# A streaming-encoder block on one core: when VectorE reads a shared PSUM bank, and how many filler products stand ahead of two places

## The chip, the cores and the metric

The kernel runs on 1 core of a Trainium2 chip. Its time is device microseconds of one execution; the time before is the median of 3 runs, 795.69 us (795.49 to 801.71). The profile is of one further execution, which took 797.75 us; its span, from the first to the last instruction in the trace, is 796.0 us.

## The reference, cut to what matters

One layer of a hybrid block: x is 512 rows of 1024. One projection gives queries, keys and values for two kinds of attention with eight heads each, an indexer and two gates.

```python
def block(args):                        # sparse heads ("a"), per 128 rows
    dots = einsum('thd,sd->ths', qib, k_idx) * IDX_DIM ** -0.5
    score = einsum('th,ths->ts', wib, relu(dots))       # indexer score
    _, sel = top_k(where(chunk ok, score, -inf), 128)   # keys each row may see
    logits = q . k[sel] * HEAD_DIM ** -0.5 + bias[bucket(sel - t)]
    return softmax(logits) @ v[sel]

a = exp(log_sigmoid(z) + later)         # stick-breaking heads ("s"): later is a
return a @ v                            # reverse running sum of log_sigmoid(-z)

x = layer_norm(ALPHA * x + merged @ w_out)              # then a gated conv MLP
```

## The kernel before, in words

All matrix work is done in pairs of high and low float parts: a weight tile of 128 x 1024 comes in by DMA from SP's queue (line 66), ScalarE makes its high part (line 93), VectorE, or GpSimd for some tiles, its low part (line 95), and TensorE then makes three products per tile of 128 (high by high, high by low, low by high; for projections lines 201 to 203, for values 224 to 226). Stream.get keeps three pieces ahead.

The phases are: a start in which the indexer's queries are projected as x arrives; the attention phase; the output projection and first norm; the MLP (lines 739 to 741 and 768 to 770); the last norm. The change touches the attention phase alone.

In that phase the order of TensorE's instructions is written by hand (manual_schedule); the order on the other engines is set by the scheduler when the program is built. The attention work of TensorE is small and waits on the other engines, so between its pieces the code puts **fillers**: products of projections, values and the branch output which are needed anyway, taken in one fixed sequence (FILL) from a generator. fill(n) issues fillers until n products are out; each step is three products, so n is rounded up to a multiple of three, and fill(16) issues 18. The total number of fillers is fixed: what is not issued at one place comes at a later one, and fill(9999) issues the rest.

The phase runs thus:

- idx_keys projects the indexer's key (ki) and splits it into kih (ScalarE, line 332) and kil (VectorE, line 333). idx_scores issues 24 pairs of products dot_ps (lines 352 and 353; the second reads kil), with fill(3) ahead of each; ScalarE takes the relu (355), VectorE adds it to score (358, 360).
- select(j) finds the 128 highest of a row of score in 16 rounds of two VectorE operations (369, 370). These rounds are spread over the fillers, and those left are issued ahead of the first sparse head.
- Sixteen heads follow, eight "s", then eight "a". For a head, start_head issues its score products (8 of them: z_ps, line 433, or l_ps, line 471), then come fill(gap), turn_weights for the head **before** (10 transposes tr_ps, line 391, then ScalarE pth 395 and VectorE ptl 396), fill(gap), weigh for that head (8 products av_ps, line 407, which read pth and ptl), and fill(gap). So a head's score products stand about 54 fillers ahead of its own transposes.
- For an s head ScalarE reads z_ps twice (keep 437, beta 438), VectorE runs the running product over keep (447) and GpSimd multiplies beta by it (449).
- For an a head VectorE adds the bias and the mask bm (made by GpSimd, line 460, from score) to l_ps and takes the row's minimum mn (475), ScalarE takes the exponential (477), VectorE scales by the reciprocal sum (480, 483).
- A pair of heads needs its queries qs and keys ks (or qa, ka): ScalarE and VectorE write their parts, and ScalarE's queue issues a DMA for the queries (306 to 308), which waits for VectorE's part.

Scores of a head lie in three PSUM banks: block 3 (512 columns) in one, **blocks 0 and 2 (128 and 384 columns) together in one**, block 1 (256) in one. These banks, those of tr_ps and that of av_ps come from one ring of four (psB); a ring place is used again only when its last reader is done.

Of the kernel before, what the change touches and what calls it, by code (L numbers as in the profile page):

```python
# [42 lines left out]
OFF = {0: 0, 2: 128, 3: 512, 1: 1024}  # L43
# [3 lines left out]
def r32(ap):  # L47
    return ap.bitcast(F32)
# [59 lines left out]
def tile_block(ctx: ExitStack, tc: tile.TileContext, xT, xN, w_qi, w_ki, w_t, w_v, w_br, w_o, w_fi, w_fo,  # L108
               bg, cw, rel, onehot, lnp, out):
    nc = tc.nc  # L110
# [8 lines left out]
    def padded(pool, shape, dt=F32, **kw):  # L119

        n = int(np.prod(shape[1:]))
        t = pool.tile([shape[0], -(-n // 32) * 32], dt, **kw)[:, :n]
        return t if len(shape) == 2 else t.rearrange("p (a b) -> p a b", a=shape[1])
# [11 lines left out]
    def pa(name):  # L135
        return psA.tile([128, 512], F32, tag="A", name=name)

    def pb(name):
        return psB.tile([128, 512], F32, tag="B", name=name)
# [36 lines left out]
    ps = pb("idle_ps")  # L176
# [80 lines left out]
    for k in range(KC):  # L257
# [9 lines left out]
        for n in range(4):  # L267
            c = slice(n * 128, n * 128 + 128)
# [56 lines left out]
    def idx_keys():  # L325
        ps = whole(proj_t("ki", M=72))
        kih = bp.tile([128, 512], F32R, tag="pt", bufs=8, name="kih")
        kil = bp.tile([128, 512], F32R, tag="pt", bufs=8, name="kil")
        wiT = bp.tile([8, 512], F32, tag="pt", bufs=8, name="wiT")
        nc.scalar.activation(wiT, ps[64:72], AF.Copy, scale=float(H) ** -0.5)  # L330
        for r in (slice(0, 64), slice(64, 128)):
            nc.scalar.activation(kih[r], ps[0:64], AF.Copy)
            nc.vector.tensor_sub(kil[r], ps[0:64], r32(kih[0:64]))
        wi = padded(cst, [128, 3, H], name="wi")
        fill(12)
        ps = pa("wi_ps")
        for j in (1, 2, 3):
            nc.tensor.transpose(ps[:, (j - 1) * H:j * H], wiT[:, j * 128:j * 128 + 128], ident[:H, :H])
        nc.vector.tensor_copy(wi.rearrange("p a b -> p (a b)"), ps[:, :3 * H])
        index["k"] = kih, kil, wi  # L340
# [3 lines left out]
    def idx_scores():  # L344
        kih, kil, wi = index["k"]
        for j in (1, 2, 3):
            N = 128 * (j + 1)
            for h in range(H):
                yield j
                ps = pa("dot_ps")  # L350
                r = slice(j * 128, j * 128 + 128)
                nc.tensor.matmul(ps[:, :N], qi[h][:, r], kih[:, :N], start=True, stop=False)
                nc.tensor.matmul(ps[:, :N], qi[h][:, r], kil[:, :N], start=False, stop=True)
                rl = bp.tile([128, 512], F32, tag="pt", bufs=8, name="relu")
                nc.scalar.activation(rl[:, :N], ps[:, :N], AF.Relu, scale=0.125)
                w = wi[:, j - 1, h:h + 1]
                if h == 0:
                    nc.vector.tensor_scalar(score[j], rl[:, :N], w, None, op0=ALU.mult)
                else:
                    nc.vector.scalar_tensor_tensor(score[j], rl[:, :N], w, score[j], op0=ALU.mult, op1=ALU.add)  # L360
# [15 lines left out]
    def select_some(n):  # L376
        for _ in zip(range(n), rounds):
            pass
# [74 lines left out]
    def dsa_head(q, k, h):  # L453
        win = bp.tile([128, 512], F32, tag="win", bufs=2, name="win")
        nc.sync.dma_start(win, s_win[h])
        nc.gpsimd.memset(win[0:64, 448:512], BIG)
        bm = padded(bp, [128, ATT + 1], tag="keep", bufs=2, name="bm")
        for j in (1, 2, 3):
            N = 128 * (j + 1)
            nc.gpsimd.tensor_add(bm[:, OFF[j]:OFF[j] + N], win[:, 512 - N:512], score[j])  # L460
        lg = bp.tile([128, ATT], F32, tag="beta", bufs=2, name="lg")
        mn = padded(bp, [128, NB], tag="mn", bufs=2, name="mn")
        sm = padded(bp, [128, NB], tag="sm", bufs=2, name="sm")
        rs = padded(bp, [128, NB], tag="rs", bufs=2, name="rs")
        for grp in ((3,), (0, 2), (1,)):
            ps = pb("l_ps")
            o = 0
            for j in grp:
                N = 128 * (j + 1)
                for hl in range(2):  # L470
                    nc.tensor.matmul(ps[:, o:o + N], q[:, hl, j * 128:j * 128 + 128], k[:, :N],
                                     start=(hl == 0), stop=(hl == 1))
                c = slice(OFF[j], OFF[j] + N)
                b = win[:, 384:512] if j == 0 else bm[:, c]
                nc.vector.tensor_tensor_reduce(out=lg[:, c], in0=ps[:, o:o + N], in1=b, scale=1.0, scalar=3.0e38,
                                               op0=ALU.add, op1=ALU.min, accum_out=mn[:, j:j + 1])
                nc.scalar.activation(lg[:, c], lg[:, c], AF.Exp, scale=-1.0, bias=mn[:, j:j + 1],
                                     accum_out=sm[:, j:j + 1])
                o += N
        nc.vector.reciprocal(rs, sm)  # L480
        for j in range(NB):
            c = slice(OFF[j], OFF[j] + 128 * (j + 1))
            nc.vector.tensor_scalar(lg[:, c], lg[:, c], rs[:, j:j + 1], None, op0=ALU.mult)
        return lg
# [45 lines left out]
    def fill(n, every=0):  # L530

        step = 0
        while n > 0:
            c = next(fillers, None)
            if c is None:
                return
            n -= c
            step += 1
            if every and step % every == 0:
                select_some(1)  # L540

    def fill_until(*keys):
        while not all(k in done for k in keys):
            fill(1)
# [5 lines left out]
    with tc.manual_schedule(engines={nc.tensor.engine}):  # L550
        fill(12)
        idx_keys()

        oh = bp.tile([64, NREL], F32R, tag="beta", bufs=2, name="oh")
        rb = edge.tile([64, H], F32R, name="rb")
        nc.gpsimd.tensor_copy(oh, ohf)
        nc.vector.tensor_copy(rb[0:32], rbf)
        nc.vector.tensor_sub(rb[32:64], rbf, r32(rb[0:32]))
        line = bp.tile([H, NREL], F32, tag="beta", bufs=2, name="line")
        for a, b in ((0, 512), (512, NREL)):  # L560
            ps = pa("line_ps")
            nc.tensor.matmul(ps[:H, :b - a], rb, oh[:, a:b], start=True, stop=True)
            nc.scalar.activation(line[:, a:b], ps[:H, :b - a], AF.Copy, scale=-1.0)
        s_line = nc.dram_tensor("s_line", (H, NREL), F32, kind="Internal").ap()
        s_win = nc.dram_tensor("s_win", (H, 128, 512), F32, kind="Internal").ap()
        nc.gpsimd.dma_start(s_line, line)
        nc.gpsimd.dma_start(s_win, bass.AP(tensor=s_line.tensor, offset=s_line.offset + 127,
                                           ap=[[NREL, H], [-1, 128], [1, 512]]))

        for j in idx_scores():  # L570
            if j > 1:
                select_some(1)
            fill(3)
# [10 lines left out]
    with tc.manual_schedule(engines={nc.tensor.engine}):  # L584
        fill_until("qs0", "ks0")
        fill(15)
        weights = start_head(0)
        sb_sticks(*weights)
        fill_until("qs1", "ks1")
        for i, (w, h) in enumerate(heads):  # L590
            gap = GAP[w]
            following = start_head(i + 1) if i + 1 < len(heads) else (None,)
            fill(gap)
            pth, ptl, lows = turn_weights(weights[0])
            if len(following) == 2:
                with tc.issue_after(lows):
                    scan = sb_sticks(*following)
                with tc.issue_after(scan):
                    select_some(1)
                fill(gap, 3)  # L600
            else:
                fill(gap)
            if h % 2 == 0:
                ytmp = bp.tile([128, 512], F32, tag="yt", bufs=2, name=f"y{w}t{h//2}")
            weigh(pth, ptl, vals[w], h, ytmp)
            if h % 2 == 1:
                (ys if w == "s" else ya).append(finish_pair(ytmp, f"y{w}{h//2}"))
            fill(gap, 3 if i < H - 1 else 0)
            weights = following
# [30 lines left out]
    for p in range(4):  # L640
        wh_wl = st.get(f"ba{p}")
        for n in (2 * p, 2 * p + 1):
            if n not in early and n not in gps:
                gps[n] = whole(proj_t(f"ga{n}"))
            ps = pb("ba_ps")
            wh, wl = wh_wl
            for k in range(4):
                c = slice((n % 2) * 512 + k * 128, (n % 2) * 512 + k * 128 + 128)
# [290 lines left out]
```

## Time and profile before

| what | value |
|---|---|
| median of 3 runs | 795.69 us |
| profiled execution | 797.75 us, span 796.0 us |
| TensorE (PE) busy | 772.2 us, 97% |
| VectorE (DVE) busy | 485.3 us, 61% |
| ScalarE (ACT) busy | 326.6 us, 41% |
| GpSimd (POOL) busy | 118.0 us, 15% |
| mean granted TensorE clock | 0.994 |
| longest wait of TensorE, by group | l_ps L471 on DVE mn L475, 10.6 us in 8 times |

In the views a line such as "PE L471 MATMUL l_ps<-ka0a,qa0a" names the engine, the line of the kernel, the operation and the tiles written and read. "[2.08 <-DVE mn L475]" behind it is the idle time of the engine just before it and the instruction that ended this idle time. The view of stretches gives, for each window of time, the busy time of PE, PE's weight loads, DVE, ACT and POOL with the number of instructions, then the granted TensorE clock (1.00 is full speed), the DMA share and the rate. In the timeline neighbouring equal instructions stand in one row with their number (x4), at the start of the first.

### The profile page before, as it was taken

The numbers are of one execution on the slowest core, as the hardware profiler recorded it, in microseconds if no ns is written. First come the engines' busy times: TensorE is split into PE (matmuls) and PEld (weight loads), VectorE is DVE, ScalarE is ACT, GpSimd is POOL, SyncE is SP. The second block draws the span as 40 slices with busy tenths as digits, with TensorE's granted clock in tenths as the row PEclk, the third lists the DMA queues.
The fourth block names the chain that finished last, engine by engine and source line by source line (L and its number), as shares of the span: only waits on it lengthen the run. The fifth ranks groups of instructions, "written<-read, shape, count | busy, mean of one in ns | idle before, by whom it ended". The sixth has DMA issues, their size and how long they took to land.

```text
span 796.0 us, 9705 instructions
## 1 busy us (share of the span) xinstructions
PE 772.2 (97%) x3696; PEld 647.0 (81%) x3696; DVE 485.3 (61%) x782; ACT 326.6 (41%) x514; POOL 118.0 (15%) x123
## 2 busy tenths in 40 slices
PE   8999999999889999999999999999999999999996
PEld 6878788888777778878889888888888888888885
DVE  5679797899657775538864554354435344545345
ACT  5565556545445547625411433333323322423300
POOL 0012464537611211000101000000000000000002
PEclk9999999999999999999999999999999999999999
DMA  7354323232212331115801332232223232231402
GB/s 253 142 182 138 96 90 107 75 113 87 85 67 93 106 119 64 69 54 174 344 11 54 107 106 86 88 119 85 100 80 112 100 106 80 105 106 57 156 26 80
DMA packets 26591, 84.01 MB, mean 106 GB/s; under 512 B 3816, under 2 KB 4200, under 8 KB 26544
## 3 DMA queue, kind: packets, MB, share of 16 engines
q1 hardware_dynamic: 22320, 72.87, 26.6%
q10 hardware_dynamic: 2576, 6.29, 2.9%
q0 software_dynamic: 1648, 4.22, 1.5%
q8 instruction: 29, 0.48, 0.2%
q14 instruction: 18, 0.15, 0.1%
HBM read 77.06 MB, written 4.21 MB: 102 GB/s over the span
## 4 chain that ended last, share of the span: by engine, by line
PE 87%; DVE 9%; ACT 1%; issue 1%; DMA 1%; POOL 0%; POOLq 0%; ACTq 0%; SPq 0%; DVEq 0%
PE d_ps L769 5%; PE d_ps L770 5%; PE d_ps L768 5%; PE u_ps L741 5%; PE u_ps L739 5%; PE g_ps L741 5%; PE u_ps L740 5%; PE g_ps L739 5%; PE g_ps L740 5%; DVE keep L447 2%; PE av_ps L407 2%; PE ga_ps L201 2%; PE ga_ps L203 2%; PE ga_ps L202 2%; PE o_ps L700 2%; PE o_ps L699 2%
## 5 line engine op out<-in xcount | busy, mean ns | idle before, releaser
L95 DVE TENSOR_TENSOR wlo<-raw,whi 128x1024 fp32r<-128x1024 f32 (+1 forms) x95 | 118.0, 1242 | 163.0 <-ACT whi L93 158.2
L93 ACT ACTIVATE whi<-raw 128x1024 fp32r<-128x1024 f32 (+1 forms) x114 | 119.8, 1052 | 206.2 <-PE d_ps L770 90.4
L739 PE MATMUL u_ps<-x1h,whi 128*128 128x512 f32 (+1 forms) x192 | 71.4, 372 | 0.0
L741 PE MATMUL u_ps<-x1h,wlo 128*128 128x512 f32 (+1 forms) x192 | 71.4, 372 | 0.0
L740 PE MATMUL u_ps<-x1l,whi 128*128 128x512 f32 (+1 forms) x192 | 71.3, 371 | 0.0
L739 PE MATMUL g_ps<-x1h,whi 128*128 128x512 f32 (+1 forms) x184 | 69.9, 380 | 0.0
L740 PE MATMUL g_ps<-x1l,whi 128*128 128x512 f32 (+1 forms) x184 | 69.9, 380 | 0.0
L741 PE MATMUL g_ps<-x1h,wlo 128*128 128x512 f32 (+1 forms) x184 | 69.9, 380 | 0.0
L768 PE MATMUL d_ps<-whi,hh 128*128 128x512 f32 (+1 forms) x178 | 65.5, 368 | 0.0
L769 PE MATMUL d_ps<-wlo,hh 128*128 128x512 f32 (+1 forms) x178 | 65.4, 368 | 0.0
L770 PE MATMUL d_ps<-whi,hl 128*128 128x512 f32 (+1 forms) x178 | 61.2, 368 | 0.0
L95 POOL TENSOR_TENSOR wlo<-raw,whi 128x1024 fp32r<-128x1024 f32 x19 | 46.9, 2469 | 46.4 <-ACT whi L93 46.4
L747 POOL MEMSET u<- 128x2 f32 x22 | 2.1, 100 | 267.8 <-DVE c L752 260.0
L740 PEld LDWEIGHTS u_ps<-x1l,whi 128*128 128x128 f32 x192 | 36.1, 188 | 6.3
L741 PEld LDWEIGHTS u_ps<-x1h,wlo 128*128 128x128 f32 x192 | 36.2, 188 | 6.2
L739 PEld LDWEIGHTS u_ps<-x1h,whi 128*128 128x128 f32 x192 | 36.2, 188 | 6.2
L740 PEld LDWEIGHTS g_ps<-x1l,whi 128*128 128x128 f32 x184 | 34.6, 188 | 6.6
L741 PEld LDWEIGHTS g_ps<-x1h,wlo 128*128 128x128 f32 x184 | 34.6, 188 | 6.6
L739 PEld LDWEIGHTS g_ps<-x1h,whi 128*128 128x128 f32 x184 | 34.6, 188 | 6.5
L753 ACT ACTIVATE c<-c,cwt 128x512 f32<-128x512 f32 x22 | 15.9, 724 | 56.5 <-DVE c L752 56.5
L769 PEld LDWEIGHTS d_ps<-wlo,hh 128*128 128x128 f32 x178 | 33.6, 189 | 5.7
L768 PEld LDWEIGHTS d_ps<-whi,hh 128*128 128x128 f32 x178 | 33.6, 188 | 5.6
(463 smaller groups left out, 1767.6 us busy)
## 6 DMA issues: line engine op xcount, KB each, us to landing
raw<-in_w_fi_dram SPq DMA_DIRECT2D x44, 512.0 KB, 3.2
raw<-in_w_t_dram SPq DMA_DIRECT2D x32, 512.0 KB, 3.3
raw<-in_w_fo_dram SPq DMA_DIRECT2D x22, 512.0 KB, 3.3
raw<-in_w_br_dram SPq DMA_DIRECT2D x8, 512.0 KB, 3.3
raw<-in_w_o_dram SPq DMA_DIRECT2D x8, 512.0 KB, 3.7
raw<-in_w_v_dram SPq DMA_DIRECT2D x7, 512.0 KB, 3.3
xr<-in_xT_dram SPq DMA_DIRECT2D x8, 256.0 KB, 5.0
raw_qi<-in_w_qi_dram SPq DMA_DIRECT2D x8, 256.0 KB, 5.0
```

Of the source, the lines that this page charges most:

```text
L93: nc.scalar.activation(hi[:, :w], t[:, :w], AF.Copy)
L95: eng.tensor_sub(lo[:, :w], t[:, :w], r32(hi[:, :w]))
L201: nc.tensor.matmul(ps[:M], wh[:, c], xh[k], start=(k == 0), stop=False)
L202: nc.tensor.matmul(ps[:M], wh[:, c], xl[k], start=False, stop=False)
L203: nc.tensor.matmul(ps[:M], wl[:, c], xh[k], start=False, stop=(k == KC - 1))
L407: nc.tensor.matmul(ps[:, 128 * i:512], vt[i][:, h].rearrange("p a d -> p (a d)"), t[i], start=(n == 0), stop=(n == len(seq) - 1))
L739: nc.tensor.matmul(ps[:, c], wh[:, kc], x1h[:, k, c], start=(k == 0), stop=False)
L740: nc.tensor.matmul(ps[:, c], wh[:, kc], x1l[:, k, c], start=False, stop=False)
L741: nc.tensor.matmul(ps[:, c], wl[:, kc], x1h[:, k, c], start=False, stop=(k == KC - 1))
L768: nc.tensor.matmul(ps, hh[f][:, r], wh[:, c], start=start, stop=False)
L769: nc.tensor.matmul(ps, hh[f][:, r], wl[:, c], start=False, stop=False)
L770: nc.tensor.matmul(ps, hl[f][:, r], wh[:, c], start=False, stop=stop)
```

## The change

Three edits, all in the attention phase:

1. In dsa_head the products and the readings of a bank are apart: for a group of blocks in one bank all products are issued first, and VectorE's readings and ScalarE's exponentials follow in a loop of their own. This differs from before only for the bank with blocks 0 and 2.
2. Ahead of the 24 indexer dots stands a fill(9).
3. Ahead of the second head's products stands fill(24), where fill_until("qs1", "ks1") stood.

```diff
@@ -464,19 +464,21 @@
             ps = pb("l_ps")
-            o = 0
+            o, parts = 0, []
             for j in grp:
                 N = 128 * (j + 1)
                 for hl in range(2):
                     nc.tensor.matmul(ps[:, o:o + N], q[:, hl, j * 128:j * 128 + 128], k[:, :N],
                                      start=(hl == 0), stop=(hl == 1))
-                c = slice(OFF[j], OFF[j] + N)
+                parts.append((j, ps[:, o:o + N]))
+                o += N
+            for j, p in parts:
+                c = slice(OFF[j], OFF[j] + 128 * (j + 1))
                 b = win[:, 384:512] if j == 0 else bm[:, c]
-                nc.vector.tensor_tensor_reduce(out=lg[:, c], in0=ps[:, o:o + N], in1=b, scale=1.0, scalar=3.0e38,
+                nc.vector.tensor_tensor_reduce(out=lg[:, c], in0=p, in1=b, scale=1.0, scalar=3.0e38,
                                                op0=ALU.add, op1=ALU.min, accum_out=mn[:, j:j + 1])
                 nc.scalar.activation(lg[:, c], lg[:, c], AF.Exp, scale=-1.0, bias=mn[:, j:j + 1],
                                      accum_out=sm[:, j:j + 1])
-                o += N
@@ -567,6 +569,7 @@
+        fill(9)
         for j in idx_scores():
@@ -586,7 +589,7 @@
         weights = start_head(0)
         sb_sticks(*weights)
-        fill_until("qs1", "ks1")
+        fill(24)
         for i, (w, h) in enumerate(heads):
```

How this moves instructions. On TensorE, in the first sparse head, with the semaphores that each row waits for (l_ps 128x512 is block 3, 128x128 block 0, 128x384 block 2, 128x256 block 1):

```order
 L471 MATMUL l_ps<-ka0a,qa0a 128x512 [waits DMAHW0_49,PE_49]
 L471 MATMUL l_ps<-ka0a,qa0a 128x512
 L471 MATMUL l_ps<-ka0a,qa0a 128x128 [waits PE_49]
 L471 MATMUL l_ps<-ka0a,qa0a 128x128
-L471 MATMUL l_ps<-ka0a,qa0a 128x384 [waits DVE_49]
-L471 MATMUL l_ps<-ka0a,qa0a 128x384
+L471 MATMUL l_ps<-ka0a,qa0a 128x384 x2
 L471 MATMUL l_ps<-ka0a,qa0a 128x256 [waits PE_49]
 L471 MATMUL l_ps<-ka0a,qa0a 128x256
```

The order of the products is as before; block 2's first product no longer waits for VectorE.

On TensorE, at the first indexer dots (vs_ps are fillers, dot_ps the dots; the row ahead of this piece is the last of line_ps):

```order
 L224 MATMUL vs_ps_163<-whi_352,xh_275 128x512
 L225 MATMUL vs_ps_163<-wlo_353,xh_275 128x512
 L226 MATMUL vs_ps_163<-whi_352,xl_276 128x512
-L352 MATMUL dot_ps<-kih,qi0a 128x256
-L353 MATMUL dot_ps<-kil,qi0a 128x256
 L224 MATMUL vs_ps_163<-whi_352,xh_302 128x512
 L225 MATMUL vs_ps_163<-wlo_353,xh_302 128x512
 L226 MATMUL vs_ps_163<-whi_352,xl_303 128x512
-L352 MATMUL dot_ps<-kih,qi0b 128x256
-L353 MATMUL dot_ps<-kil,qi0b 128x256
```

The first dot stood behind three fillers and now stands behind twelve; every later dot stands nine fillers later too, and the last of the 24 behind the whole of ks0.

Between the first head's and the second head's score products stood 33 fillers (6 of qs1, 24 of ks1, 3 of qs2), and now stand 24; from there on every piece of attention work stands nine fillers earlier. The second head's products thus come ahead of the last six of ks1. On ScalarE, around the second head (keep and beta read its z_ps, ks1a and ks1b are the second pair's keys, the DMA row waits for VectorE's qs1b):

```order
 L306 ACTIVATE qs1b<-qs_ps 64x512
+L437 ACTIVATE keep<-z_ps 128x512
+L438 ACTIVATE beta<-z_ps 128x512
 L308 DMA qs1b<-qs1b 64x1024
+L437 ACTIVATE keep<-z_ps 128x512
+L438 ACTIVATE beta<-z_ps 128x512
+L437 ACTIVATE keep<-z_ps 128x256
+L438 ACTIVATE beta<-z_ps 128x256
 L93 ACTIVATE whi_896<-raw_894 128x1024
 L295 ACTIVATE ks1a<-ks_ps 64x512
 L296 ACTIVATE ks1b<-ks_ps 64x512
-L437 ACTIVATE keep<-z_ps 128x512
```

The readings of the second head's banks stood behind a split (whi) and the keys' two copies, and now stand ahead of them. The rest of the scheduler's order moves in many places by a row or a few; the number of ScalarE's table loads stays at 10.

## The prediction

> **What bounds the kernel now.** I read the page first: its busy times and its chain of work that ended last.
>
> ```profile
> PE 772.2 (97%) x3696; PEld 647.0 (81%) x3696; DVE 485.3 (61%) x782; ACT 326.6 (41%) x514; POOL 118.0 (15%) x123
> PE 87%; DVE 9%; ACT 1%; issue 1%; DMA 1%; POOL 0%; POOLq 0%; ACTq 0%; SPq 0%; DVEq 0%
> ```
>
> TensorE is busy for 772.2 of 796.0 us and has 87% of the chain. The change takes no product away, so all it can win is TensorE's idle 23.8 us and any time at a reduced clock. Next, TensorE's waits, by whom they waited for (us in total, times, longest):
>
> ```profile
> PE l_ps L471 <- DVE mn L475: 10.6, 8, 2.1
> PE tr_ps L391 <- ACT beta L438: 1.1, 2, 0.8
> PE dot_ps L353 <- DVE kil L333: 1.0, 1, 1.0
> PE av_ps L407 <- DVE ptl L396: 0.7, 1, 0.7
> PE dot_ps L352 <- ACT kih L332: 0.2, 1, 0.2
> ```
>
> The first group is the largest by far: once in each of the eight sparse heads TensorE stands between blocks 0 and 2 until VectorE has read block 0. Then the view of stretches (busy us with counts for PE, PEld, DVE, ACT, POOL, then granted clock, DMA share, GB/s):
>
> ```profile
> 95.00:160.00 65.00, 65.00 (x326) 55.08 (x325) 56.77 (x105) 37.16 (x67) 35.61 (x20) 1.00 0.28 90
> 160.00:201.00 41.00, 39.87 (x199) 33.64 (x197) 38.96 (x65) 20.96 (x36) 22.30 (x12) 1.00 0.33 103
> 201.00:220.00 19.00, 17.83 (x80) 14.80 (x80) 12.20 (x24) 10.35 (x20) 11.21 (x10) 0.91 0.21 70
> 220.00:240.00 20.00, 17.84 (x80) 14.78 (x80) 11.35 (x24) 9.78 (x20) 3.28 (x4) 0.91 0.20 67
> 240.00:258.00 18.00, 16.54 (x82) 13.96 (x83) 13.15 (x28) 8.68 (x17) 3.53 (x4) 1.00 0.31 102
> 275.00:293.00 18.00, 16.17 (x80) 13.61 (x80) 13.15 (x25) 8.48 (x18) 4.08 (x4) 1.00 0.22 74
> ```
>
> Three things are to be seen: the stick heads (95 to 201) leave TensorE no idle time to win but for 1.1 us; VectorE is nearly full there (38.96 of 41 us at the end); and the clock is 0.91 in two stretches, at the first two sparse heads, and 1.00 elsewhere.
>
> **Part 1, the bank of blocks 0 and 2.** The timeline of TensorE at the waits: one whole group of score products, and the restarts of three more heads.
>
> ```profile
> 255.94 0.79 PE L471 MATMUL l_ps<-ka1b,qa1b 128*128 128x512 f32 x4
> 257.67 0.85 PE L471 MATMUL l_ps<-ka1b,qa1b 128*128 128x384 f32 x4 [0.94 <-DVE mn L475]
> 258.36 0.39 PE L201 MATMUL qa_ps<-xh,whi 128*128 128x512 f32 x1
> 201.96 0.87 PE L471 MATMUL l_ps<-ka0a,qa0a 128*128 128x384 f32 x4 [2.08 <-DVE mn L475]
> 221.85 0.87 PE L471 MATMUL l_ps<-ka0b,qa0b 128*128 128x384 f32 x4 [2.06 <-DVE mn L475]
> 293.03 0.85 PE L471 MATMUL l_ps<-ka2b,qa2b 128*128 128x384 f32 x4 [1.86 <-DVE mn L475]
> ```
>
> The same eight shapes without a wait stand in the stick heads:
>
> ```profile
> 76.75 1.43 PE L433 MATMUL z_ps<-ks0a,qs0a 128*128 128x512 f32 x8
> 78.02 0.39 PE L201 MATMUL qs_ps<-xh,whi 128*128 128x512 f32 x1
> ```
>
> Eight products take 78.02 - 76.75 = 1.27 us from start to the next start. With the wait it is 258.36 - 255.94 = 2.42, so 1.15 us is lost where the wait shows 0.94: 0.21 more, for the pipeline that has to fill again. Over eight heads that is 10.6 + 8 x 0.21 = **12.3 us**. In the changed program these products have no wait for VectorE, so this comes back unless another wait takes its place. VectorE's reading of block 0 now waits for block 2's product too, some 0.2 us, and nothing on TensorE hangs on that before the transposes.
>
> **Part 2, the clock.** The two stretches at 0.91 lose 0.09 x 19 = 1.7 and 0.09 x 20 = 1.8 us. They follow the waits of 2.08 and 2.06 us; after the one of 1.86 us the clock stays 1.00. So I take the halved clock as the price of a gap over about 2 us, and **3.5 us** more come back if no gap as long comes anew. Bounds: 0, if the gaps are not the cause, to 3.5. [...] I follow the rows, since two of two gaps over 2 us are followed by a slow stretch and no other gap is.
>
> **Part 3, nine fillers ahead of the dots.**
>
> ```profile
> 40.70 0.39 PE L225 MATMUL vs_ps<-wlo,xh 128*128 128x512 f32 x1
> 40.93 0.40 PE L226 MATMUL vs_ps<-whi,xl 128*128 128x512 f32 x1
> 41.53 0.38 PE L352 MATMUL dot_ps<-kih,qi0a 128*128 128x256 f32 x1 [0.21 <-ACT kih L332]
> 42.90 0.39 PE L353 MATMUL dot_ps<-kil,qi0a 128*128 128x256 f32 x1 [0.98 <-DVE kil L333]
> 43.12 0.40 PE L224 MATMUL vs_ps<-whi,xh 128*128 128x512 f32 x1
> ```
>
> A filler takes 0.23 us from start to start, a dot of half the columns about 0.12. Lost here: 0.60 - 0.23, 1.37 - 0.12 and 0.22 - 0.12, together 1.7 us. Nine fillers are 2.1 us, so the first dot would start at 43.2 instead of 41.16, when kil has been read at 42.90: all **1.7 us** come back. The dots then come some 0.4 us later than before, and the nine fillers return later; the same number of products stands ahead of the first head's scores.
>
> **Part 4, the second head.** Fewer fillers stand there now, 24 for 33, so its scores and the first head's transposes come 9 x 0.23 = 2.1 us earlier. These transposes waited already:
>
> ```profile
> 90.94 0.60 PE L391 MATMUL tr_ps<-ident,beta 128*128 128x128 f32 x4
> 92.32 0.66 PE L391 MATMUL tr_ps<-ident,beta 128*128 128x128 f32 x4 [0.78 <-ACT beta L438]
> 93.30 0.44 PE L391 MATMUL tr_ps<-ident,beta 128*128 128x128 f32 x2 [0.33 <-ACT beta L438]
> 85.25 2.45 POOL L449 TENSOR_TENSOR beta<-beta,keep 128x1280 f32<-128x1280 f32 x1 [1.81 <-DVE keep L447]
> 85.52 0.68 DVE L307 SCALAR_TENSOR_TENSOR qs1a<-qs_ps,qs1a 64x512 fp32r<-64x512 f32 x1
> 87.56 0.69 DVE L307 SCALAR_TENSOR_TENSOR qs1b<-qs_ps,qs1b 64x512 fp32r<-64x512 f32 x1
> 91.67 0.59 ACT L438 ACTIVATE beta<-z_ps 128x512 f32<-128x512 f32 x1
> ```
>
> The second and third group of transposes need banks of the second head's scores, which ScalarE frees (the first at 92.26); ScalarE is held by a DMA that waits for VectorE's qs1a (done 86.2) and qs1b (88.25). The wait of 1.1 us with two refills is about 1.5 lost. Now TensorE arrives at 90.94 - 1.7 - 2.1 = 87.1. ScalarE frees the banks earlier, since a split and two key copies no longer stand ahead: after 86.2 come qs1b, keep and beta (some 0.6 each), so the first bank is free at about 88.5; after 88.25 come a DMA issue, keep and beta, so the second is at about 90.1. With VectorE where it was, TensorE loses about 2.4 us there, and up to 0.5 at the products behind; as VectorE does some value splits earlier in its idle places I take 2.0. Against 1.5 that is a loss of **0.5 us** (bounds: a loss of 1.5 with VectorE 0.5 later; a gain of 1.4 with no wait left). The input beta itself is ready at 87.7, no later than the banks.
>
> **Part 5, what is late next.** The first sparse head waits for the last rounds of the selection:
>
> ```profile
> 201.27 0.43 DVE L372 TENSOR_SCALAR score<-score 128x512 f32<-128x512 f32 x1
> 207.17 3.36 DVE L483 TENSOR_SCALAR lg<-lg,rs 128x128 f32<-128x128 f32 x4
> 210.45 1.61 DVE L396 TENSOR_TENSOR ptl<-tr_ps,pth 128x512 fp32r<-128x512 f32 x3
> 213.61 0.39 PE L407 MATMUL av_ps<-pth,vs 128*128 128x512 f32 x1
> ```
>
> From 201.27 VectorE works with little idle time to the end of ptl at 212.06; TensorE needs the first part of ptl (211.1) at 213.6. Now TensorE is ahead by 2.1 (fillers) and 1.2 (parts 3 and 4), so its scores start at 195.8 instead of 199.08, and 1.3 + 4.1 + 1.1 + 4.1 us of products later, at 206.4, it wants ptl. VectorE saves its 0.8 us of waiting for block 2 (the restart at 201.96), and can move forward by what it idled in 160 to 201 (2.0 us) and part of the 8.2 us in 95 to 160; I take 2.0 of these. Then ptl is there at 211.1 - 2.8 = 208.3, and TensorE loses some 1.9, part of it perhaps already at the transposes, whose banks free with the same readings. I take **a loss of 1.8 us** (bounds 0.4 and 3.8).
>
> In the other seven sparse heads TensorE's period is 1.3 + 54 x 0.23 + 1.1 + 1.2 = 16.0 us, and VectorE's work 13.15 us in windows of 18. VectorE has 5 us from a head's scores to the transposes that take their banks over; the longest wait so far (2.1) fits in it. I take a loss of **0.7 us** for all (bounds 0 to 2).
>
> **Sum.** 12.3 + 3.5 + 1.7 - 0.5 - 1.8 - 0.7 = **14.5 us**. The profiled execution would go from 797.75 to 783.2 (span 781.5), the median from 795.69 to **781.2 us**. The profiled execution stands 2.06 us over the median of the runs shown; should one slow stretch of it be missing in those, the gain on the median is 1.7 smaller. With the bounds this case runs from 777 to 786.5.
>
> **The rivals.**
>
> *A wait at the transposes or at av_ps in every sparse head.* Banks and weights still come from VectorE, a head later. For it: VectorE's queue mixes these readings with splits that wait for ScalarE, and 1 to 2 us were lost so in each head. Against it: 13.15 of 16 us of work, and 5 us of slack. At 0.8 us in each of eight heads, 6.4 us go back: 787.6 us.
>
> [...]
>
> *Slower: VectorE becomes the bound of the stick heads.* It does 56.77 us of work in 65, or 14.0 per head of 16.0 us, and TensorE's pieces now press 2 to 3 us earlier on it, with each head's transposes waiting for its running product. It decides if VectorE needs more than 16.0 us per head; to eat the gain it would have to need 17.8 in all eight, at 3 us of wait each 24 us go: 805 us. Against it: the work is the same, and TensorE waits nowhere in 95 to 160.
>
> *It does not do what it says*: TensorE still stands at the bank, 796 us. Against it: the wait is gone from the program.
>
> **How the numbers follow.** Chances: the forecast 0.75, waits in every sparse head 0.12, clock stays 0.08, slower 0.03, nothing 0.02. A measurement here can tell about 1% from no change, 8.0 us, so faster means under 787.7 us. That takes nearly all of the first case, half of the second and all of the third: 0.88. Within 1%: 0.09; slower: 0.03. The range of 777 to 788 holds the first case, the third and half of the second.
>
> **What would show it.** Right: no wait of l_ps on mn; score products of 1.3 us in all eight heads; clock 1.00 from 195 to 240; no wait at the first dots; a wait of some 2 us at the second head's time on z_ps's readers, and one at the first sparse head on ptl. [...]

## The result, and the profile after

| | before | after |
|---|---|---|
| median | 796.07 us (795.44 to 801.71, 6 runs) | 784.51 us (784.44 to 787.92, 6 runs) |
| profiled execution | 797.75 us, span 796.0 | 784.44 us, span 782.7 |
| ratio of the runs | | 0.9847 [0.981, 0.9885] |

The forecast was 781.2 us (777.0 to 788.0), faster. The kernel is faster, by 1.5% (the interval leaves out 1), inside the range and 3.3 us over the forecast. The profiled executions differ by 13.3 us, the medians by 11.2 (against the 795.69 of the first runs), because the profiled execution of before stood 2.06 us over its median and that of after at the lowest of its runs.

The page of after, busy times and the chain of work that ended last:

```profile
PE 768.4 (98%) x3696; PEld 644.5 (82%) x3696; DVE 479.9 (61%) x782; ACT 324.7 (41%) x514; POOL 118.0 (15%) x123
PE 93%; DVE 3%; ACT 2%; issue 1%; POOL 0%; POOLq 0%; ACTq 0%
```

TensorE holds 93% of the chain instead of 87%, and VectorE 3% instead of 9%. TensorE's waits in after (us in total, times, longest):

```profile
PE tr_ps L391 <- ACT beta L438: 2.4, 3, 1.8
PE va_ps L224 <- DVE qa1b L307: 1.6, 1, 1.6
PE av_ps L407 <- DVE ptl L396: 1.0, 2, 0.7
PE l_ps L471 <- DVE ka2a L297: 0.2, 1, 0.2
```

The 10.6 us of l_ps on mn are gone, and so are both waits of the dots. Two rows are new in size: transposes that wait 1.8 us for ScalarE's readings of z_ps, and a filler that waits 1.6 us for VectorE. The stretches of after (PE, PEld, DVE, ACT, POOL busy, then clock):

```profile
95.00:160.00 65.00, 62.89 (x314) 52.92 (x312) 55.94 (x107) 35.80 (x64) 32.20 (x20) 1.00 0.28 90
195.00:215.00 20.00, 20.00 (x101) 16.86 (x100) 10.28 (x25) 11.10 (x20) 13.82 (x12) 1.00 0.32 102
215.00:235.00 20.00, 20.00 (x100) 16.94 (x100) 14.63 (x33) 12.74 (x23) 3.47 (x4) 1.00 0.27 85
```

At the first sparse heads TensorE is busy without a break and at full clock, where before it had 17.8 of 19 and 20 us at 0.91. The loss has moved to 95 to 160, where it now idles 2.1 us. TensorE's timeline in after, at the first dots, at a sparse head's scores and at the two new waits:

```profile
42.28 0.39 PE L226 MATMUL vs_ps<-whi,xl 128*128 128x512 f32 x1
42.51 0.28 PE L352 MATMUL dot_ps<-kih,qi0a 128*128 128x256 f32 x1
42.63 0.28 PE L353 MATMUL dot_ps<-kil,qi0a 128*128 128x256 f32 x1
42.75 0.39 PE L224 MATMUL vs_ps<-whi,xh 128*128 128x512 f32 x1
87.77 0.44 PE L391 MATMUL tr_ps<-ident,beta 128*128 128x128 f32 x2 [0.26 <-ACT beta L438]
105.71 0.66 PE L391 MATMUL tr_ps<-ident,beta 128*128 128x128 f32 x4 [1.78 <-ACT beta L438]
194.09 0.47 PE L224 MATMUL va_ps<-whi,xh 128*128 128x512 f32 x1 [1.64 <-DVE qa1b L307]
198.30 1.43 PE L471 MATMUL l_ps<-ka0a,qa0a 128*128 128x512 f32 x8
```

The dots follow each other at 0.12 us; the eight score products stand in one row (x8) without a wait. At 105.71 it is the transposes of the **second** stick head that wait, for banks of the third head's scores. (A head's own transposes stand 72 fillers behind its scores, four gaps of 18, and not about 54 as written ahead; 54 lie between one head's scores and the next head's.) Why ScalarE frees them so late stands in its own timeline:

```profile
92.48 0.59 ACT L306 ACTIVATE qs2a<-qs_ps 64x512 fp32r<-64x512 f32 x1
99.17 0.47 ACTq L308 DMA_DIRECT2D qs2a<-qs2a  x1
99.69 0.59 ACT L306 ACTIVATE qs2b<-qs_ps 64x512 fp32r<-64x512 f32 x1 [6.62 <-DVE score L370]
104.57 0.60 ACT L437 ACTIVATE keep<-z_ps 128x512 f32<-128x512 f32 x1
105.07 0.59 ACT L438 ACTIVATE beta<-z_ps 128x512 f32<-128x512 f32 x1
```

ScalarE stands still for 6.62 us. The view names VectorE's score as releaser, the last event before the restart, but the row above tells the reason: next in ScalarE's queue is the DMA of the queries, and it needs VectorE's qs2a. VectorE's timeline has that late:

```profile
93.27 4.64 DVE L447 TENSOR_TENSOR_SCAN keep<-keep,first 128x128 f32<-128x128 f32 x4
98.48 0.66 DVE L307 SCALAR_TENSOR_TENSOR qs2a<-qs_ps,qs2a 64x512 fp32r<-64x512 f32 x1
189.68 2.95 DVE L447 TENSOR_TENSOR_SCAN keep<-keep,first 128x128 f32<-128x128 f32 x4
193.25 0.69 DVE L307 SCALAR_TENSOR_TENSOR qa1b<-qa_ps,qa1b 64x512 fp32r<-64x512 f32 x1
196.91 0.43 DVE L372 TENSOR_SCALAR score<-score 128x512 f32<-128x512 f32 x1
```

In the changed program qs2a and qa1b stand behind the four running products of the next head, qs2a behind 4.64 us of them and qa1b behind 2.95. qa1b is the last reader of a PSUM bank from the fillers' ring (psA) that va_ps needs: that is the second new wait.

### The profile page after: what moved, and what is told of

Same layout as the page of the kernel before. It is cut to its first block, busy times and chain, and to the rows that moved or that the text cites. A ratio compares the mean times of both kernels' runs of the same rounds, so it can differ in the third digit from the quotient of the medians.

```text
span 782.7 us, 9703 instructions
## 1 busy us (share of the span) xinstructions
PE 768.4 (98%) x3696; PEld 644.5 (82%) x3696; DVE 479.9 (61%) x782; ACT 324.7 (41%) x514; POOL 118.0 (15%) x123
## 4 chain that ended last, share of the span: by engine, by line
PE 93%; DVE 3%; ACT 2%; issue 1%; POOL 0%; POOLq 0%; ACTq 0%
PE d_ps L771 5%; PE d_ps L772 5%; PE d_ps L773 5%; PE u_ps L742 5%; PE u_ps L744 5%; PE g_ps L742 5%; PE u_ps L743 5%; PE g_ps L744 5%; PE g_ps L743 5%; PE av_ps L407 2%; PE ga_ps L201 2%; PE ga_ps L203 2%; PE ga_ps L202 2%; PE o_ps L703 2%; PE o_ps L702 2%; PE o_ps L701 2%
## 5 line engine op out<-in xcount | busy, mean ns | idle before, releaser
L95 DVE TENSOR_TENSOR wlo<-raw,whi 128x1024 fp32r<-128x1024 f32 (+1 forms) x95 | 115.8, 1220 | 155.4 <-ACT whi L93 150.9
```

Of the source, the lines that this page charges most:

```text
L95: eng.tensor_sub(lo[:, :w], t[:, :w], r32(hi[:, :w]))
```

## The experiments

Ratios are to runs of the kernel before on the same chip, with 95% intervals. The runs come from four groups, in which the median of the kernel before was 796.1 (the change), 796.5, 797.9 and 798.1 us, so a difference of times between two groups is uncertain by up to 2 us.

My theory after the result: edit 1 gave back the waits at the bank and, with them, the slow stretches; edit 2 gave back the dots; edit 3 (24 fillers for 33) cost time, because it moved VectorE's part of the queries behind running products. The rival was that edit 3 does its share and the new waits would come in any case, as TensorE runs ahead.

### Which edit does what

*Edit 1 alone* (before, with the new loop in dsa_head):

> Edit 1 alone: a bank's readings follow all its products, and the fillers stand as before. My account: nearly all of the gain is this edit (12.3 us of waits in eight heads, up to 3.5 us of clock), and edit 3 costs more than it gives, through VectorE's order. So 783 us, within 1.5 us of the changed kernel or faster; l_ps waits nowhere on mn, the dots wait 1.2 us and the first transposes 1.1 us as before, and neither the 1.8 us wait of the second stick head's transposes nor the 1.6 us wait of va_ps is there. Rival: the fillers are what makes room, and without them the wait moves to tr_ps or av_ps in the sparse heads: 788 us or more.

Measured: 782.69 us, ratio 0.9824 [0.9799, 0.9849]. No wait of l_ps on mn, and the waits at the dots (1.2) and at the first transposes (1.1) as before. Edit 1 alone is not slower than the whole change. Its profile has one stretch at half clock, and that was not expected. The view of stretches of this kernel, cut at the step of the clock:

```profile
38.22:41.64 3.42, 2.23 (x11) 1.15 (x11) 2.36 (x4) 2.39 (x4) 0.46 (x1) 1.00 0.52 156
41.64:45.05 3.41, 3.41 (x11) 2.83 (x12) 0.84 (x2) 0.77 (x2) 0.80 (x2) 0.50 0.47 160
```

The gaps ahead of it were 0.21 and 0.98 us, at the dots. So "a gap over about 2 us" is not the condition.

*Edits 2 and 3 alone:*

```diff
+        fill(9)
         for j in idx_scores():
...
-        fill_until("qs1", "ks1")
+        fill(24)
```

> Edits 2 and 3 alone: nine fillers ahead of the dots, 24 ahead of the second head's products, and the banks read as before. My account: 1.7 us come back at the dots and about 1 at the first transposes, and 2.4 at the next head's transposes and 1.8 at va_ps are lost, so 796 to 798 us against 795.5, with the eight waits of l_ps on mn still there. Rival (the two edits win by themselves what they take away, 1.7 + 1.5 us): 792.5 us.

Measured: 794.65 us, ratio 0.9971 [0.9956, 0.9987], between the two numbers. Its waits:

```profile
PE l_ps L471 <- DVE mn L475: 7.8, 8, 1.4
PE tr_ps L391 <- ACT beta L438: 2.1, 2, 1.7
PE va_ps L224 <- DVE qa1b L307: 1.6, 1, 1.6
```

The l_ps waits are 7.8 us instead of 10.6, since at the first two sparse heads TensorE now comes later against VectorE, which has ended its selection earlier; the waits at tr_ps and va_ps stand against that. The new waits come with edit 3 whether edit 1 is there or not.

*Edits 1 and 2, edit 3 undone* (the change with `fill_until("qs1", "ks1")`):

> The changed kernel with edit 3 undone (the fillers up to the end of ks1 ahead of the second head's products, 33 as before). My account: VectorE's qs2a is then again ahead of the next running product, ScalarE's queue is not held by the query DMA, and the waits of 1.8 us at tr_ps and 1.6 us at va_ps go; the 1.1 us wait at the first transposes comes back: 781.5 us against 784.5. Rival: those two waits are the price of TensorE being earlier, whatever the fillers, and stay: 785.5 us or more.

Measured: **780.53 us**, ratio 0.9795 [0.9767, 0.9823]. Neither new wait is there; only the first transposes wait (1.4 us). The third edit costs 784.5 - 780.5 = 4.0 us. VectorE's timeline of this kernel shows the difference in order:

```profile
94.29 0.68 DVE L307 SCALAR_TENSOR_TENSOR qs2a<-qs_ps,qs2a 64x512 fp32r<-64x512 f32 x1 [0.57 <-ACT qs2a L306]
95.23 3.90 DVE L447 TENSOR_TENSOR_SCAN keep<-keep,first 128x128 f32<-128x128 f32 x4
```

qs2a goes ahead of the running products, and comes 4.2 us earlier than in after. Little of that reaches the banks, though: ScalarE is then held by the second DMA of the pair, and its readings of the first bank come only 1.1 us earlier than in after.

```profile
100.54 0.47 ACTq L308 DMA_DIRECT2D qs2b<-qs2b  x1
103.94 0.59 ACT L438 ACTIVATE beta<-z_ps 128x512 f32<-128x512 f32 x1
106.60 1.25 PE L391 MATMUL tr_ps<-ident,beta 128*128 128x128 f32 x10
```

The other 3.3 us are TensorE's: it comes to the second head's transposes at 106.60 instead of 103.33. So at this wait the order is the smaller part. At va_ps it is nearly all: qa1b starts at 188.64 instead of 193.25, and TensorE comes only 0.6 us later (193.08 for 192.45).

### The price of the bank in two halves

*The old interleaving in the first two sparse heads, the rest as changed:*

```diff
+            def read(j, p):
+                ...
             for j in grp:
...
+                if h < 2:
+                    read(j, ps[:, o:o + N])
...
```

> The changed kernel, but in the first two sparse heads a block is read ahead of the next block's products, as before. If gaps of over 2 us halve the clock: where the wait comes back at over 2 us it is followed by a stretch of 3.4 us at half clock, 1.7 us each, so up to 784.5 + 4.6 + 3.4 = 792.5 us, and with shorter waits no slow stretch: 787 to 789 us. Rival (the slow stretches belong to the place or come by themselves): two slow stretches near the first two sparse heads whatever the length of the wait, 790 us or more, or slow stretches elsewhere.

Measured: 785.89 us, ratio 0.9862 [0.9837, 0.9887], a little under the least that I had expected. The two waits are 0.5 and 0.9 us, not 2.1: TensorE comes there later against VectorE than before. No slow stretch follows. So the old order at that place does not bring slow stretches by itself, which speaks for the long gaps; and the size of a wait belongs to how far ahead of VectorE TensorE is.

*The old interleaving in the last six* (the same with h >= 2):

> The changed kernel with the old interleaving of products and readings in the last six sparse heads (the complement of the run with the old first two, which cost 1.4 us at waits of 0.5 and 0.9 us). My account, that each head pays its wait and 0.21 us of refill: before, these six waited 0.9, 1.9, and four times about 0.9, so 6 to 8 us more than the changed kernel, 790.5 to 792.5, and with waits under 1.95 us a slow stretch at most by chance (1.7 us). Rival: the readings of the last six are hidden anyway, since the second head's wait was mostly VectorE's lateness from the selection, so less than 4 us, under 788.5.

Measured: 792.02 us, ratio 0.993 [0.9908, 0.9951], in the band of my account. Its waits:

```profile
PE l_ps L480 <- DVE mn L472: 6.4, 6, 1.4
```

With 0.21 us of refill each these make 6.4 + 1.3 = 7.7 us, and that is what the six pieces lose in the trace from start to start (15.4 us for 6 x 1.27). The time rose by 792.0 - 784.5 = 7.5, or 6.6 by the two ratios. The term "wait plus refill" holds.

### Where the third edit loses

*The nine fillers put behind the second head's products:*

```diff
+            late9 = 9 if i == 0 else 0
             following = start_head(i + 1) if i + 1 < len(heads) else (None,)
-            fill(gap)
+            fill(gap + late9)
```

> The changed kernel, but the nine fillers taken away ahead of the second head's products are put behind them (24 ahead, 27 instead of 18 behind), so that the second head's products stay early and everything behind the first head's transposes stands where it stood with fill_until. My account: the two new waits (tr_ps 1.8 us at the second stick head's transposes, va_ps 1.6 us at 194) come from the later pieces standing nine fillers early, which puts VectorE's qs2a and qa1b behind running products and selections; so both vanish, and the time is 780.5 to 781.5, as with banks and dots alone (780.53). Rival: the cost of the third edit comes from the second head's products being issued early (they take the banks and ScalarE's time); then at least one wait of 1.5 us or more stays near the first or second head's transposes and the time is 783 or more.

Measured: 780.01 us, ratio 0.9781 [0.9757, 0.9806]. The time is a little under the band. Both waits are gone, and that at the first transposes too. It isn't the second head's early products that cost; it is that all that follows stands nine fillers early.

*30 fillers instead of 24:*

> The changed kernel with 30 fillers ahead of the second head's products (24 in the change, 33 with fill_until). In the program VectorE's qs2a still stands behind the running products, and qa1b behind one of three ptl instead of behind two. My account, that the place in VectorE's order costs the time and not how many fillers are missing: the tr_ps wait stays at 1.5 to 2.0 us though six fillers (1.4 us) have come back; the va_ps wait falls to 1.0 or less; time 782.5 to 783.8. Rival, a wait that shrinks with each filler put back: tr_ps 0.4 us or less and va_ps 0.3 or less, time 780.5 to 781.5.

Measured: 782.59 us, ratio 0.9818 [0.9792, 0.9845]. The time is the expected one, and va_ps no longer waits, but the tr_ps wait isn't where I had it. The row of tr_ps in this kernel:

```profile
PE tr_ps L391 <- ACT beta L438: 1.8, 2, 1.5
```

The 1.5 us stand at the **first** transposes (restart at 89.53 us), and a step at half clock follows them in this profile:

```profile
87.34:90.75 3.41, 1.63 (x13) 1.06 (x11) 1.38 (x2) 3.37 (x8) 2.28 (x2) 1.00 0.13 29
90.75:94.17 3.42, 3.42 (x10) 2.69 (x9) 2.64 (x5) 2.46 (x5) 0.00 (x0) 0.50 0.42 152
```

ScalarE is held behind the query DMA again, for 5.21 us, and reads the third head's z_ps from 104.86 on, as late as in after. The second transposes don't wait all the same, since TensorE now comes to them at 107.29 instead of 103.33: six fillers, the first wait and the slow step later. So the place of qs2a in VectorE's order does not decide alone; it is the order and how early TensorE comes. This part of my account was too simple. Part of what the two waits gave back went into the longer wait at the first transposes and the slow step.

*The DMA of the queries on GpSimd's queue:*

```diff
-            nc.scalar.dma_start(r32(t[oth]), r32(t[own]))
+            nc.gpsimd.dma_start(r32(t[oth]), r32(t[own]))
```

> The changed kernel, with the DMA of the queries (line 308) issued from GpSimd's queue instead of ScalarE's; VectorE's order is the same, qs2a still behind the running products and qa1b behind ptl. My account: the 1.8 us at the second stick head's transposes come from ScalarE, which stood 6.6 us in its own queue behind that DMA; so the tr_ps wait goes (0.3 us or less left), while the va_ps wait of 1.6 us, which comes from VectorE holding a PSUM bank, stays at 1.2 to 1.8. Time 782 to 783 (784.45 less 1.8 and two refills). Rival: VectorE's lateness itself is what TensorE waits for there, whoever issues the DMA: both waits stay, time 784 to 785. A third: GpSimd, held by the DMA in turn, brings beta late, and TensorE waits at tr_ps for GpSimd instead: 784 or more.

Measured: 779.87 us, ratio 0.9777 [0.9748, 0.9807], better than I had expected: both waits are gone. ScalarE's timeline in this kernel:

```profile
91.06 0.58 ACT L306 ACTIVATE qs2a<-qs_ps 64x512 fp32r<-64x512 f32 x1
96.07 0.59 ACT L306 ACTIVATE qs2b<-qs_ps 64x512 fp32r<-64x512 f32 x1 [4.43 <-DVE qs2a L307]
99.48 0.60 ACT L437 ACTIVATE keep<-z_ps 128x512 f32<-128x512 f32 x1
```

ScalarE still stands 4.43 us, now because qs2b waits for qs2a, but it reaches keep at 99.48 instead of 104.57, ahead of the transposes at 102.04, which no longer wait. For va_ps the expectation was wrong in its premise. I had taken VectorE's order for unchanged, but qa1b now stands ahead of the running products:

```profile
185.66 0.69 DVE L307 SCALAR_TENSOR_TENSOR qa1b<-qa_ps,qa1b 64x512 fp32r<-64x512 f32 x1
186.72 2.96 DVE L447 TENSOR_TENSOR_SCAN keep<-keep,first 128x128 f32<-128x128 f32 x4
```

VectorE's qs2a also starts 3.1 us earlier here (95.38 instead of 98.48), as the running products ahead of it begin earlier and take 2.96 us instead of 4.64; why they are shorter stays open. Of the 5.1 us that keep comes earlier, 3.6 are the earlier restart behind qs2a and 1.5 the second DMA, which no longer holds ScalarE. So the run shows that the DMA in ScalarE's queue is a part of the cause of the first wait, and not how large a part of the 6.62 us it is; the second wait it removes by another order, not by the queue alone.

*Edits 1 and 2 with that DMA moved:*

> Edits 1 and 2 with fill_until kept, and the queries' DMA issued from GpSimd's queue. The question is whether the two ways of losing the new waits add up to a version better than either (780.5 without the third edit; 779.9 with it and the DMA moved). My account: with fill_until the only wait left ahead of the last head is that at the first transposes (1.1 us with its refill 1.3 to 1.7), and it comes from ScalarE standing behind the query DMA; moved away it goes, so 778.8 to 779.8. Rival: that wait is VectorE's lateness, it stays, 780.3 to 780.8.

Measured: **778.9 us** (778.07 to 779.24), ratio 0.9762 [0.9742, 0.9782], as my account had it, and the lowest time of this study, though its interval overlaps those of the two runs with 780.01 and 779.87 us. Its waits:

```profile
PE idle_ps L178 <- DVE idle L175: 1.2, 1, 1.2
PE av_ps L407 <- DVE ptl L396: 0.7, 1, 0.7
PE av_ps L407 <- ACT pth L395: 0.4, 1, 0.4
```

and its busy times on the page:

```profile
PE 766.4 (99%) x3696; PEld 644.0 (83%) x3696; DVE 479.8 (62%) x782; ACT 325.9 (42%) x514; POOL 128.1 (17%) x139
```

No wait is left between the products at the start (idle_ps) and the last head, behind which no filler stands.

### When does the clock fall?

Each of the two slow stretches in before lasts 3.413 us (from 202.75 and from 223.23 us). They lie 20.48 us apart, 6.0 times 3.413, and the two in the run of edits 2 and 3 163.84, 48.0 times: in these traces they are steps of one grid. To see what decides, I added 19 stretches behind the attention phase of the kernel with edits 1 and 2, with nothing left out (shown cut):

```diff
+        ...
+        for n, wide in GAPS:
+            for _ in range(32):
+                nc.tensor.matmul(ps, xh[0][:, :128], xh[1], start=True, stop=True)
+            nc.scalar.activation(pr[:, :128], ps[:, :128], AF.Copy)
+            for _ in range(n):
+                nc.scalar.activation(pr[:, :wide], r32(pr[:, :wide]), AF.Copy)
+            nc.tensor.matmul(ps, pr[:, :128], xh[1], start=True, stop=True)
```

> The kernel with banks and dots alone, and behind its attention phase 19 added stretches: 32 products of 512 columns, then a chain of 2 to 9 copies on ScalarE for which TensorE stands idle, so gaps of some 0.6 to 4 us; nothing of the block is left out. The question is which gap is followed by a stretch at half clock. Three theories. (A) The prediction's: every gap over 2 us is followed by one, none below. (B) A whole idle window of 3.4 us is needed: only gaps over 3.4 us, and of those up to 6.8 us only some. (C) What I read in the runs so far: the slow stretches of a run lie on a fixed grid of 3.413 us (two of them 48.0 and 6.0 such steps apart), and a step runs at half clock if in the step before TensorE streamed nothing for more than about 2.0 us in sum (five steps with 2.14 to 2.52 us were followed by one, none of those with 1.93 or less). By (C) gaps up to 1.9 us are never followed by one, gaps of 2.1 to 3.4 us in some cases and not in others, according to how the grid cuts them, gaps over 4.0 us always; and the count of lost time in the step before decides in all 19.

> The kernel with the added gaps once more, unchanged. In the first look 14 of the 19 gaps stood bare, between 1.79 and 4.01 us: the two of 1.79 were followed by no half clock; of the three of 2.22 two were, of the three of 2.66 to 2.67 one, those of 2.13, 2.41 and 2.47 not, those of 3.11, 3.56 and 4.01 were. If the grid of 3.413 us runs free of the program, it stands elsewhere against the gaps this time: some of the gaps of 2.1 to 2.7 us change sides, those of 1.79 stay free, those of 3.56 and 4.01 stay followed, and the sum without streaming in the step before still separates all (followed at about 2.0 us or more, not below). If instead something in the gap itself decides (what waits, what comes behind), the same gaps are followed as in the first look.

The two runs (986.67 and 981.06 us with the added work) gave 14 bare gaps each, of the same lengths at the same places. (The second expectation miscounts the first run: all three of 2.22 us were followed there.)

| gap, us | followed by half clock, first run | second run |
|---|---|---|
| 1.79 | 0 of 2 | 1 of 2 |
| 2.13 | 0 of 1 | 1 of 1 |
| 2.22 | 3 of 3 | 0 of 3 |
| 2.41, 2.47 | 0 of 2 | 0 of 2 |
| 2.66, 2.67 | 1 of 3 | 0 of 3 |
| 3.11 | 1 of 1 | 1 of 1 |
| 3.56 | 1 of 1 | 0 of 1 |
| 4.01 | 1 of 1 | 1 of 1 |

The first gap of 2.22 us, in the first run, in steps of that run's grid:

```profile
409.27:412.68 3.41, 1.19 (x6) 0.69 (x5) 0.00 (x0) 1.94 (x5) 0.00 (x0) 1.00 0.00 0
412.68:416.09 3.41, 3.41 (x9) 2.66 (x9) 0.00 (x0) 0.00 (x0) 0.00 (x0) 0.50 0.00 0
```

and the same gap in the second run:

```profile
410.18:413.60 3.42, 1.63 (x8) 1.01 (x6) 0.00 (x0) 1.57 (x5) 0.00 (x0) 1.00 0.00 0
413.60:417.01 3.41, 2.99 (x13) 2.50 (x14) 0.00 (x0) 0.37 (x1) 0.00 (x0) 1.00 0.00 0
```

The same gap lies within one step there (1.19 us busy, then half clock) and is cut by the grid here (1.63 and 2.99 busy, full clock). Theory A, a gap over 2 us, falls at once, and so does B: gaps of 2.2 us are followed, and one of 3.56 is not. C holds in the main, with two misses of mine: one gap of 1.79 us was followed, and that of 3.56 was not, as the grid cut it nearly in halves (1.61 and 1.66 us busy in its two steps). I counted for each step of all 13 traces at full clock and ahead of the tail (some 2850 steps) the time without streaming, a product of 512 columns as 0.227 us, shorter ones in proportion, and a transpose as the 0.11 us at which transposes follow each other. (Counted by its columns alone, as half of that, several steps with transposes would have about 2.1 us and no half clock behind them, so here transposes count as work.) 18 steps had 2.14 us or more, and all were followed by half clock. The six between 2.03 and 2.13 were followed in three cases. None of the others, some 2830, up to 1.98, was. These bounds move by some 0.05 us with the place of the streaming within a product's row. A step of 3.413 us at half clock cost 1.6 us in before: from the end of the first sparse head's scores to the transposes TensorE took 5.73 us there, and 4.12 in after.

## Why the prediction was right, and where it was not

The terms, worked out from starts to starts in the profiled executions (each place against the same sequence without a wait):

| step | predicted, us | measured, us |
|---|---|---|
| Part 1, bank of blocks 0 and 2 | 12.3 | 12.3 |
| Part 2, clock | 3.5 | 3.2 |
| Part 3, dots | 1.7 | 1.7 |
| Part 4, first head's transposes and weights | -0.5 | +0.7 |
| next head's transposes | none | -2.5 |
| Part 5, first sparse head on ptl | -1.8 | 0 |
| va_ps on qa1b | none | -1.8 |
| other sparse heads | -0.7 | -1.0 |
| start of the kernel (not of the change) | none | +0.7 |
| sum | 14.5 | 13.3 |

**Part 1 was right**, and the runs with edit 1 alone and with the old interleaving in two and in six heads show it. Its size is not a constant of the kernel, though: at the places where TensorE stands after edits 2 and 3 the same interleaving costs 1.4 + 7.5 = 8.9 us by the times of the two runs, and 7.8 + 8 x 0.21 = 9.5 by the waits of the run of edits 2 and 3.

**Part 2 was right in its sum and wrong in its reason.** The slow stretches went with the gaps, so the case in which the clock stays, with its chance of 0.08, did not come: the two stretches of before at 0.91 are at 1.00 in after. That holds beyond the one profile: the granted clock was 0.996 to 0.998 in the six runs of the change and 0.988 to 0.996 in 13 runs of before, and one slow step, 3.413 us at half clock in a span of 796, is 0.002 of it. But the condition "over about 2 us" came from two rows, and the probe broke it: its three gaps of 2.22 us were all followed by half clock in one run and none of them in the next. What went with half clock was the time without streaming in the step of 3.413 us before: 2.14 us or more in 18 steps of 18. How many slow steps one execution has varied, though (from 0.988 to 0.996 it is four), and the profiled one of before stood 2.06 us over its median: of the 3.3 us over the forecast, 2.1 come from taking the gain of one profile for that of the median, a case that the sum had named with 1.7.

**Part 3 was right.** The dots start at 42.51 at 0.12 us each.

**Part 4 is the step that failed.** It said that the second head's products come early and the first head's transposes pay with 2.0 us "as VectorE does some value splits earlier". They paid 0.5, and the products behind them 0.4, since VectorE was not where it had been: its qs1a started at 83.36 instead of 85.52. The wait came one head later, by the mechanism that Part 4 had described for qs1a and qs1b, a DMA that holds ScalarE's queue until VectorE has made its part. I followed the moved instructions to one head only. Every later piece stands nine fillers early too, and with it the scheduler put the third and the sixth pair's VectorE parts (qs2a, qa1b) behind running products of 4.64 and 2.95 us. Against the run without edit 3 the first of the two waits comes mostly from TensorE being earlier (3.3 us of 4.4), the second from the order. Together they are 2.5 + 1.8 = 4.3 us of loss that the sum lacks; the run without edit 3, in which neither stands, is 4.0 us faster.

**Part 5 gave nearly the right loss for the wrong reason.** No wait on ptl came at the first sparse head. VectorE ended its selection at 197.3 instead of 201.7, 4.4 us earlier where I had taken 2.0 (2.8 by the end of ptl), and TensorE, held by the two new waits, began the scores at 198.3 and not at 195.8. Of the six kernels without these two waits (edit 1 alone, edits 1 and 2, nine fillers behind, 30 fillers, and the two with the DMA moved), one shows the ptl wait again: with the third edit kept and the DMA moved it is 0.7 us.

The first rival (a wait in every sparse head) and the slower one (VectorE as the bound of the stick heads) are not there: TensorE idles 2.1 us in 95 to 160, in one place. That the range held is luck in part: 4.3 us of loss that I had not named fell inside the bounds of losses that I had, and the 1.8 us of Part 5 that did not come made room for it.

## What to carry to other kernels

Reading a PSUM bank only when all products into it are out cost nothing here, where the readers had slack (edit 1 alone gave 0.9824), and it took away a wait in each of eight heads. When pieces of a hand-made order move, follow every engine's moved instruction through all later rounds of the loop, above all a DMA in the queue of an engine that also frees PSUM: it made ScalarE wait here for VectorE, which makes the DMA's data (a part of the 6.62 us at the first DMA of qs2, and 1.37 at the second). And a slow stretch in one profile was a draw here, not a fixed price (behind the three gaps of 2.22 us it came three times in one run and never in the next): take it from several executions, or count the idle time per step of the grid, 3.413 us here.

## What the runs showed of the hardware

In these 13 traces the granted clock of TensorE changed on a grid of 3.413 us, which stood elsewhere from run to run: the probe had steps from 409.27 us in its first run and from 410.18 in its second. By the count above all 18 steps with 2.14 us or more without streaming were followed by a step at half clock, three of the six with 2.03 to 2.13 us, and none with up to 1.98, be that one gap or several short ones: 0.21 and 0.98 us of waiting, with their refills and the short products around them, were enough in the run of edit 1 alone. In before TensorE was busy through both half-clock steps (from 202.75 and from 223.23 us), and the clock was 1.00 in the step behind each. In the first run of the probe it was busy for 2.16 us of a step at half clock (from 467.30 us), and the step behind it was at half clock too. Behind the first gap of 2.22 us the same 32 products took 9.01 us in the first run and 7.43 in the second, 1.6 us less.
